# Turning the accumulated stick-breaking values by plain transposes, with the two halves added on VectorE

## The chip, the cores and the metric

The kernel runs on one core of one Trainium2 chip. Its metric is the device time of one execution in microseconds (us), taken as the median of several executions. The changed kernel is measured in the same way. Within the core, TensorE multiplies matrices into PSUM (its partial-sum memory), VectorE and ScalarE read PSUM and work on SBUF (the core's working memory), GpSimd works on SBUF, and SyncE's queue issues the transfers between DRAM and SBUF. In the rows of the profile these are PE (with PEld for its weight loads), DVE, ACT, POOL and SP.

## The reference, cut to what matters

The reference is one layer of a decoder over 2048 tokens of width 1024. A normalised input is projected to the inputs of four mixers. Their outputs are normalised, put side by side and projected back. A feed-forward part (gate, up and down products) follows. The change lies in one mixer, the stick-breaking attention with four heads of width 64:

```python
z = einsum('bqhd,bkhd->bhqk', qblk, kh) * scale
log_1m = where(causal, log_sigmoid(-z), 0.0)
tail = cumsum(log_1m, reverse=True) - log_1m
w = where(causal, exp(log_sigmoid(z) + tail), 0.0)
out = einsum('bhqk,bkhd->bqhd', w, vh)
```

For every query the keys before it are weighted, and `out` is the weighted sum of the values. The kernel reaches float32 accuracy with a faster rounded number format by carrying each operand as two parts, a rounded high part and a remainder.

## The kernel before, in words

The program has two stages. In the first, up to about 780 us, the projections and the four mixers run interleaved. In the second come the output projection and the feed-forward part. The change touches only the first.

The stick-breaking attention (function `stick`) is called 8 times: for 2 pairs of heads, and in each pair for 4 chunks of 512 queries. One call walks over its 2 heads and, for each, over the blocks of 512 keys from the nearest back to the first. For each block:

- `weights` multiplies queries by keys into a PSUM tile `z` (L325, L326). ScalarE takes two sigmoids (L329 into `tfix`, L332 into `s`). VectorE forms the running product with a scan (L338, tile `pr`) and multiplies (L343).
- `turn` transposes the weights with TensorE (L353, tile `tr`, four transposes of 128x128 at a time). ScalarE writes the high part (L355) and VectorE the remainder (L356), tile `wt`.
- `values` multiplies by the stacked values (L364, L365) and accumulates in a PSUM tile `acc`. The values of one head are held as 128 columns, 64 of the high part and 64 of the remainder, so `acc` has 128 rows: the sum for the high part above the sum for the remainder.

After the last block of a head, `finish` runs. ScalarE copies `acc` to SBUF (L371, tile `accs`). TensorE multiplies each 128 queries of it by `stack`, two identities of 64 one above the other (L374): this turns the tile and adds its two halves in one product. The result `yp` (128 queries by 4 times 64) is copied by ScalarE into `ysb` (L376). Two heads and 4 chunks in 2 pairs make 16 calls of `finish`. `acc` and `yp` share one PSUM bank: their pool tag has a single buffer, so the next head's `acc` cannot start before `yp` has been read. At the end of a call, two transfers store `ysb` to DRAM (`yd<-ysb`).

`stick` is one generator of work. A second one, `feed`, yields the projections and the other mixers, and `merge` draws from both with a ratio for each call. That gives the order of the program. A scheduler of the framework then reorders the instructions of each engine by its own estimate of times, so a changed instruction can move others far away from it. All transfers go through one issuing queue in order (L121). In the rows, `ps<-h,w_k` and the like are projections (L265 to L267, L277 to L279); `z<-ck,cq` (L468), `o<-block` (L510) and the loads `qr<-cd` and `kr<-cd` belong to the sliding-window mixer, whose operands GpSimd splits (L460, L461, tile `cq`).

Of the kernel before, what the change touches and what calls it, by code (L numbers as in the profile page):

```python
# [9 lines left out]
F32 = mybir.dt.float32  # L10
F32R = mybir.dt.float32r
AF = mybir.ActivationFunctionType
ALU = mybir.AluOpType
PSUM = bass.MemoryType.PSUM

P = 128
# [5 lines left out]
HD = 64  # L22
# [15 lines left out]
def _t5_bucket(dist):  # L38
    df = np.maximum(dist, 1).astype(np.float32)
    large = 16 + (np.log(df / np.float32(16)) / np.float32(math.log(8.0)) * np.float32(16)).astype(np.int32)  # L40
    return np.where(dist < 16, dist, np.minimum(large, 31))


def _constants():
    c = {}
    c["ident"] = np.eye(P, dtype=np.float32)
    c["ones"] = np.ones((P, P), np.float32)
    c["stack"] = np.concatenate([np.eye(HD, dtype=np.float32)] * 2, 0)
    j = np.arange(384)
    dist = 255 - j  # L50
    inside = (dist >= 0) & (dist < P)
    b = _t5_bucket(np.clip(dist, 0, P - 1))
    oh = np.zeros((32, 384), np.float32)
    oh[b[inside], j[inside]] = 1.0
    c["onehot"] = oh
    c["outside"] = np.where(inside, 0.0, NEG).astype(np.float32)[None, :]

    tok, out = np.arange(P)[:, None], np.arange(P)[None, :]
    band, first, before = (np.zeros((P, 2, 2, n), np.float32) for n in (P, P, 16))
    for g, w in enumerate((2, 4, 8, 16)):  # L60
        inside = ((out >= tok) & (out - tok < w)).astype(np.float32)
        band[:, g // 2, g % 2] = inside / np.float32(w) - (out == tok)
        first[:, g // 2, g % 2] = inside / np.minimum(out + 1, w).astype(np.float32) - (out == tok)
        before[:, g // 2, g % 2] = ((out + P - tok < w) / np.float32(w))[:, :16]
    c["band"] = np.concatenate([band.reshape(P, -1), before.reshape(P, -1)], 1)
    c["band0"] = first.reshape(P, -1)
    return c


def _layout(inputs):  # L70
# [30 lines left out]
    for n, v in _constants().items():  # L101
        a["c_" + n] = v
# [9 lines left out]
def build(nc, tc, A):  # L112
    with ExitStack() as top:
        _build(nc, tc, A, top)


def _build(nc, tc, A, top):
    V, S, G = nc.vector, nc.scalar, nc.gpsimd

    def load(out, in_):  # L120
        nc.sync.dma_start(out, in_)  # L121
# [19 lines left out]
    ident = const.tile([P, P], F32, name="ident")  # L141
# [28 lines left out]
    with ExitStack() as ph1:  # L170
        fas = ExitStack()
        fa = fas.enter_context(tc.tile_pool(name="feeda", bufs=2, side="left", reuse_waits="tile"))
        c1 = ph1.enter_context(tc.tile_pool(name="c1", bufs=1, side="left"))
        sb = ph1.enter_context(tc.tile_pool(name="sb", bufs=2, side="left"))

        stack = c1.tile([P, HD], F32, name="stack")
        tfix = [c1.tile([P, CH + 1], F32, name=f"tfix{i}") for i in range(2)]
        for t in tfix:
            G.memset(t[:, CH:CH + 1], 1.0)
# [133 lines left out]
        def stick(c, pair, q):  # L313
            ysb = sb.tile([P, 4, 2, HD], F32, name="ysb", tag="ysb", bufs=1)
# [44 lines left out]
            def values(h, j, kb, r, wt):  # L359
                vs = vstack[:, 4 * j + kb, h, :]  # L360
                first = j == c and kb == 0
                if first:
                    acc[h] = psum.tile([P, CH], F32, name="acc", tag="acc", bufs=1)
                nc.tensor.matmul(acc[h][:, r], vs, wt[:, 0, r], start=first, stop=False)  # L364
                nc.tensor.matmul(acc[h][:, r], vs, wt[:, 1, r], start=False, stop=j == 0 and kb == 3)  # L365
                if j == 0 and kb == 3:
                    finish(h)

            def finish(h):
                accs = sb.tile([P, CH], F32, name="accs", tag="accs", bufs=1)  # L370
                S.copy(accs, acc[h])  # L371
                yp = psum.tile([P, CH], F32, name="yp", tag="acc", bufs=1)
                for i in range(4):
                    nc.tensor.matmul(yp[:, i * HD:(i + 1) * HD], accs[:, i * P:(i + 1) * P], stack,  # L374
                                     start=True, stop=True)
                S.copy(ysb[:, :, h, :], yp[:, :4 * HD].rearrange("p (i d) -> p i d", d=HD))  # L376

            groups = [(h, j) for h in range(2) for j in range(c, -1, -1)]
            prev, late = None, None
# [356 lines left out]
        def new_q():  # L736
            return [sb.tile([P, 2, CH], F32R, name="dq", tag="dq", bufs=4) for _ in range(2)]
# [44 lines left out]
        def feed():  # L782
# [9 lines left out]
            w_v = split_w(A["w_v"], "w_v", "wv", 1)  # L792
            w_b = [split_w(A["w_b"][:, 4 * t:4 * t + 4], f"w_b{t}", eng=V, k0=4 * t) for t in range(2)]
            spare.clear()
            load(stack, A["c_stack"])
            q[0] = new_q()
            pool = mixer_b()
            for s in range(NS):
                c = s // 2
# [6 lines left out]
                h = hs.pop(s) if s else hs.pop(0)  # L806
# [72 lines left out]
            for s in range(NS):  # L879
                h = hs.pop(s)  # L880
# [16 lines left out]

        sw = []
        source = feed()
        reached = [0]  # L900

# [24 lines left out]
        for n in range(2 * NCH):  # L926
            c, pair = n % NCH, n // NCH
# [206 lines left out]
```

## Time and profile before

| | |
|---|---|
| median of 3 runs | 2396.13 us (2395.85 to 2400.73) |
| the profiled execution's own time | 2402.21 us |
| its span | 2400.5 us |
| mean granted TensorE clock | 0.974 of full speed |
| TensorE busy in the span | 2271.7 us (95%) |
| VectorE busy | 1505.8 us (63%) |
| ScalarE busy | 1024.8 us (43%) |
| first stage, mixers | up to about 780 us |

The profiled execution is 6.1 us above the median of the runs, so a sum made from its rows is a difference to be taken from the median. A share of busy time is a mean over stages: TensorE is near full use in the second stage, while the first has waits on VectorE and on transfers. The granted clock is given as a share of full speed (2.4 GHz); 0.5 is the lower of its two levels.

### The profile page before, as it was taken

The numbers are of one execution on the slowest core, as the hardware profiler recorded it, in microseconds if no ns is written. First come the engines' busy times: TensorE is split into PE (matmuls) and PEld (weight loads), VectorE is DVE, ScalarE is ACT, GpSimd is POOL, SyncE is SP. The second block draws the span as 40 slices with busy tenths as digits, with TensorE's granted clock in tenths as the row PEclk, the third lists the DMA queues.
The fourth block names the chain that finished last, engine by engine and source line by source line (L and its number), as shares of the span: only waits on it lengthen the run. The fifth ranks groups of instructions, "written<-read, shape, count | busy, mean of one in ns | idle before, by whom it ended". The sixth has DMA issues, their size and how long they took to land.

```text
span 2400.5 us, 31011 instructions
## 1 busy us (share of the span) xinstructions
PE 2271.7 (95%) x11432; PEld 1915.6 (80%) x11432; DVE 1505.8 (63%) x2467; ACT 1024.8 (43%) x2176; POOL 278.8 (12%) x356
## 2 busy tenths in 40 slices
PE   6999999998977899989999999999999999999998
PEld 6989888887865787768888888888888888888886
DVE  4356989887675455567666666644576666653443
ACT  5556656664455243343333333533333333333332
POOL 4222423441122120100000000000000000000000
PEclk9999999998977999999999999999999999999999
DMA  7534322333532245753222223665432222234553
GB/s 278 190 130 171 139 89 88 106 103 112 192 105 91 100 139 162 234 186 98 91 92 80 79 79 125 200 201 168 146 104 84 79 86 89 87 107 141 186 174 123
DMA packets 141001, 314.05 MB, mean 131 GB/s; under 512 B 12688, under 2 KB 68400, under 8 KB 134704
## 3 DMA queue, kind: packets, MB, share of 16 engines
q1 hardware_dynamic: 140848, 312.06, 38.8%
q8 instruction: 90, 1.47, 0.2%
q14 instruction: 63, 0.52, 0.1%
HBM read 229.44 MB, written 82.58 MB: 130 GB/s over the span
## 4 chain that ended last, share of the span: by engine, by line
PE 73%; DMA 10%; DVE 8%; ACT 4%; issue 3%; POOL 2%; SPq 1%; DVEq 0%; POOLq 0%; ACTq 0%
PE dn L1081 20%; PE gb L1025 15%; PE gc L1025 10%; PE ga L1025 10%; DVE pr L338 2%; PE ops L728 2%; PE ops L730 2%; PE ops L729 2%; DMA y<-yd 1%; DVE s L343 1%; DMA qr<-cd 1%; DMA xt<-in_x 1%; PE ps L277 1%; PE ps L278 1%; PE ps L279 1%
## 5 line engine op out<-in xcount | busy, mean ns | idle before, releaser
L1081 PE MATMUL dn<-wd,act 128*128 128x512 f32 x2112 | 479.5, 389 | 0.0
L1081 PEld LDWEIGHTS dn<-wd,act 128*128 128x128 f32 x2112 | 396.5, 188 | 82.4
L1025 PE MATMUL gb<-T,fw 128*128 128x512 f32 x1584 | 388.2, 394 | 0.0
L1025 PEld LDWEIGHTS gb<-T,fw 128*128 128x128 f32 x1584 | 297.5, 188 | 68.5
L1025 PE MATMUL ga<-B,fw 128*128 128x512 f32 x1056 | 259.5, 394 | 0.0
L1012 ACT CAST fw<-fsum 128x512 fp32r<-128x512 f32 x176 | 108.4, 619 | 308.4 <-DVE fsum L1008 162.3
L1025 PEld LDWEIGHTS ga<-B,fw 128*128 128x128 f32 x1056 | 198.6, 188 | 45.9
L975 DVE TENSOR_TENSOR wd<-wr,wd 128x512 fp32r<-128x512 f32 x176 | 115.2, 689 | 186.4 <-ACT wd L1075 186.2
L1075 ACT CAST wd<-wr 128x512 fp32r<-128x512 f32 x176 | 102.0, 619 | 236.5 <-DMA wr<-in_w_down 208.8
L149 POOL TENSOR_TENSOR fr<-rs_t,mhalf 128x1 f32<-128x1 f32 x32 | 21.5, 674 | 1433.1 <-DVE rs_t L148 1428.2
L975 DVE TENSOR_TENSOR fw<-fsum,fw 128x512 fp32r<-128x512 f32 x176 | 120.9, 690 | 36.4 <-ACT fw L1012 36.0
L1025 PE MATMUL gc<-T,fw 128*128 128x512 f32 x528 | 131.6, 397 | 5.8 <-DVE T L975 5.8
L338 DVE TENSOR_TENSOR_SCAN pr<-tfix,cr 128x513 f32<-128x513 f32 x96 | 126.1, 1323 | 11.4 <-ACT tfix L329 11.1
L1025 PE MATMUL gc<-B,fw 128*128 128x512 f32 x528 | 128.0, 391 | 0.0
L1025 PEld LDWEIGHTS gc<-T,fw 128*128 128x128 f32 x528 | 100.6, 191 | 28.7 <-DVE T L975 6.2
L728 PE MATMUL ops<-wo,yT 128*128 128x512 f32 x256 | 105.7, 413 | 11.5 <-ACT yT L656 10.8
L1025 PEld LDWEIGHTS gc<-B,fw 128*128 128x128 f32 x528 | 99.2, 188 | 21.7
L343 DVE TENSOR_TENSOR s<-s,pr 128x512 f32<-128x512 f32 (+3 forms) x152 | 107.9, 717 | 10.8 <-POOL s L335 4.5
L356 DVE TENSOR_TENSOR wt<-tr,wt 128x512 fp32r<-128x512 f32 (+3 forms) x160 | 94.1, 601 | 29.5 <-ACT wt L355 29.3
L1012 ACT CAST fw<-fraw 128x512 fp32r<-128x512 f32 x132 | 81.7, 621 | 66.9 <-DVE fw L975 32.4
L730 PE MATMUL ops<-wo,yT 128*128 128x512 f32 x256 | 102.7, 407 | 3.4 <-DVE yT L657 3.4
L729 PE MATMUL ops<-wo,yT 128*128 128x512 f32 x256 | 104.2, 408 | 0.0
(234 smaller groups left out, 4499.0 us busy)
## 6 DMA issues: line engine op xcount, KB each, us to landing
fraw<-in_w_gu SPq DMA_DIRECT2D x88, 512.0 KB
wr<-in_w_down SPq DMA_DIRECT2D x88, 512.0 KB
h<-hd SPq DMA_DIRECT2D x32, 1024.0 KB
actd<-up SPq DMA_DIRECT2D x88, 256.0 KB
ar<-actd SPq DMA_DIRECT2D x88, 256.0 KB
hd<-h SPq DMA_DIRECT2D x16, 1024.0 KB
xr<-in_xT SPq DMA_DIRECT2D x16, 512.0 KB
xt<-in_x SPq DMA_DIRECT2D x16, 512.0 KB
```

The lines of the kernel that those rows point to most:

```text
L277: nc.tensor.matmul(o, hk[:, 0], w(k, 0), start=k == 0, stop=False)
L338: V.tensor_tensor_scan(pr[:, c0:][:, ::-1], t[:, c0:][:, ::-1], t[:, c0:][:, ::-1], carry[h][i], op0=ALU.mult, op1=ALU.bypass)
L343: (G if (4 * pair + c, i) in ON_G else V).tensor_tensor(w[:, c0:], w[:, c0:], pr[:, c0 + 1:], op=ALU.mult)
L356: V.tensor_tensor(wt[:, 1, r], tr[:, r], wt[:, 0, r].bitcast(F32), op=ALU.subtract)
L728: nc.tensor.matmul(ps, yk[:, 0, :], wo[k][half][:, 0], start=k == 0, stop=False)
L729: nc.tensor.matmul(ps, yk[:, 0, :], wo[k][half][:, 1], start=False, stop=False)
L730: nc.tensor.matmul(ps, yk[:, 1, :], wo[k][half][:, 0], start=False, stop=k == KT - 1)
L975: V.tensor_tensor(dst, src, hi.bitcast(F32), op=ALU.subtract)
L1012: S.copy(w[:, 0], src)
L1025: nc.tensor.matmul(bank, w[:, wi, sl], hc[n][:, k, hi], start=start and k + wi + hi == 0, stop=stop and k == 3 and wi == 1, skip_group_che ...
L1075: S.copy(w[n][:, 0], wr[:, n])
L1081: nc.tensor.matmul(pss[2 * i + n], a[:, ai, t], w[n][:, wi], start=f + ai + wi == 0, stop=f == NF - 1 and ai == 1)
```

## The change

The four products with `stack` (64 columns each) become four transposes of 128x128 with the identity, which is in SBUF anyway for `turn`. `yp` then holds, for each 128 queries, 64 columns of the high sum and 64 of the remainder's. ScalarE copies the first half into `ysb`, as wide as before, reading runs of 64 columns. VectorE then adds the second half from PSUM. The tile `stack`, its constant and its transfer go.

```diff
-    c["stack"] = np.concatenate([np.eye(HD, dtype=np.float32)] * 2, 0)
...
-        stack = c1.tile([P, HD], F32, name="stack")
...
                 S.copy(accs, acc[h])
                 yp = psum.tile([P, CH], F32, name="yp", tag="acc", bufs=1)
                 for i in range(4):
-                    nc.tensor.matmul(yp[:, i * HD:(i + 1) * HD], accs[:, i * P:(i + 1) * P], stack,
-                                     start=True, stop=True)
-                S.copy(ysb[:, :, h, :], yp[:, :4 * HD].rearrange("p (i d) -> p i d", d=HD))
+                    nc.tensor.transpose(yp[:, i * P:(i + 1) * P], accs[:, i * P:(i + 1) * P], ident)
+                ypv = yp.rearrange("p (i u d) -> p i u d", i=4, u=2)
+                S.copy(ysb[:, :, h, :], ypv[:, :, 0])
+                V.tensor_tensor(ysb[:, :, h, :], ypv[:, :, 1], ysb[:, :, h, :], op=ALU.add)
...
-            load(stack, A["c_stack"])
```

The scheduler moves other work too. On VectorE the order of the multiplication of `wraw` (L250) and of `dg` (L206), from which `rbc` is made, is exchanged near the start. Lines of the changed kernel stand 1 or 2 lower than the same lines before. Three places matter later.

On the transfers' queue, near the start of the program: loads of weights (`wraw`) and of the input (`xr`, `xt`), and the store of a row of scales (`rbcd<-rbc`, made by ScalarE). Before:

```order
L121 DMA stack<-in_c_stack 128x64
L121 DMA cw<-in_pool_w 64x64
L121 DMA hd_0_76<-h 128x2048
...
L121 DMA wraw<-in_w_b 128x1024
L121 DMA xr<-in_xT 128x4x256
L121 DMA rbcd_193<-rbc 128x256
L121 DMA xr<-in_xT 128x4x256
L121 DMA vd_68<-vt 128x2x256
```

And now:

```order
L120 DMA cw<-in_pool_w 64x64 x2
L120 DMA hd_0_76<-h 128x2048
...
L120 DMA wraw<-in_w_b 128x1024
L120 DMA rbcd_193<-rbc 128x256
L120 DMA xr<-in_xT 128x4x256 x2
L120 DMA xt<-in_x 128x1024
```

The load of `stack` is gone, a second small load of `cw` now stands ahead of the stores of `h`, and the first load of `xr` stands behind the store of `rbc`.

On VectorE at the 14th `finish` (about 625 us before); `pr` is the scan, `s` the product after it, `st` a projection's result. Before:

```order
L356 TENSOR_TENSOR wt<-tr,wt 128x512
L356 TENSOR_TENSOR wt<-tr,wt 128x384
L885 TENSOR_TENSOR st<-ps,rbc 128x256
L338 SCALAR_TENSOR_TENSOR pr<-tfix_221,cr 128x513
L343 TENSOR_TENSOR s<-s,pr 128x512
L338 SCALAR_TENSOR_TENSOR pr<-tfix_222,cr 128x513
L885 TENSOR_TENSOR st<-ps,rbc 128x256
```

And now:

```order
L354 TENSOR_TENSOR wt<-tr,wt 128x512
L354 TENSOR_TENSOR wt<-tr,wt 128x384
L883 TENSOR_TENSOR st<-ps,rbc 128x256
L336 SCALAR_TENSOR_TENSOR pr<-tfix_220,cr 128x513
L341 TENSOR_TENSOR s<-s,pr 128x512
L336 SCALAR_TENSOR_TENSOR pr<-tfix_221,cr 128x513
L375 TENSOR_TENSOR ysb<-yp,ysb 128x4x64
L336 SCALAR_TENSOR_TENSOR pr<-tfix_220,cr 128x513
```

The new addition stands between two scans, and the instruction behind it is a scan on which the next weights wait.

On TensorE at the 13th `finish` (about 571 us before), with the sliding-window products `z<-ck,cq` around it. Before:

```order
L353 MATMUL tr<-ident,s 128x128 x2
L468 MATMUL z<-ck,cq 128x128 x2
L468 MATMUL z<-ck,cq 128x256 x2
L325 MATMUL z<-kstack_226,dq 128x512
L326 MATMUL z<-kstack_226,dq 128x512
L353 MATMUL tr<-ident,s 128x128 x2
L468 MATMUL z<-ck,cq 128x128
L468 MATMUL z<-ck,cq 128x256
L325 MATMUL z<-kstack_226,dq 128x512
L326 MATMUL z<-kstack_226,dq 128x512
L374 MATMUL yp<-stack,accs 128x64 x4
L468 MATMUL z<-ck,cq 128x128 x3
```

And now:

```order
L351 MATMUL tr<-ident,s 128x128 x2
L323 MATMUL z<-kstack_225,dq 128x512
L324 MATMUL z<-kstack_225,dq 128x512
L351 MATMUL tr<-ident,s 128x128 x2
L467 MATMUL z<-ck,cq 128x128 x3
L263 MATMUL ps<-h,w_c 128x256
L264 MATMUL ps<-h,w_c 128x256
L265 MATMUL ps<-h,w_c 128x256
L323 MATMUL z<-kstack_225,dq 128x512
L324 MATMUL z<-kstack_225,dq 128x512
L372 MATMUL yp<-ident,accs 128x128 x4
L467 MATMUL z<-ck,cq 128x256 x4
```

The sliding-window products stand later and in larger groups, with projections `ps<-h,w_c` between them (21 more of these stand a little ahead of the piece shown).

## Rows read from the trace of the kernel before

**Rows 1.** The page, part 1: busy time of each engine.

```profile
PE 2271.7 (95%) x11432; PEld 1915.6 (80%) x11432; DVE 1505.8 (63%) x2467; ACT 1024.8 (43%) x2176; POOL 278.8 (12%) x356
```

**Rows 2.** Windows: length, then PE, PEld, DVE, ACT, POOL busy, clock, DMA share, GB/s.

```profile
60.00:270.00 210.00, 204.71 (x1382) 192.33 (x1381) 124.30 (x209) 126.66 (x293) 52.70 (x62) 0.98 0.44 155
270.00:540.00 270.00, 254.23 (x1538) 220.06 (x1537) 239.21 (x414) 170.88 (x395) 106.07 (x128) 1.00 0.31 105
```

**Rows 3.** Chain of work that ended last: start, length, what.

```profile
13.33 9.05 DMA wraw<-in_w_v
...
106.86 0.92 PE yp L374 x8
...
206.00 0.44 PE tr L353 x4
...
496.17 0.84 PE yp L374 x8
...
752.89 0.87 PE tr L353 x4
758.92 1.72 PE yp L374 x8
760.66 0.38 ACT ysb L376
```

**Rows 4.** Groups by shape: busy us, mean ns, idle before and releaser.

```profile
L338 DVE TENSOR_TENSOR_SCAN pr<-tfix,cr 128x513 f32<-128x513 f32 x96 | 126.1, 1323 | 11.4 <-ACT tfix L329 11.1
L353 PE MATMUL tr<-ident,s 128*128 128x128 f32 x544 | 95.2, 281 | 9.3 <-DVE s L343 5.1 <-DVE wt L356 4.0
L343 DVE TENSOR_TENSOR s<-s,pr 128x512 f32<-128x512 f32 x104 | 84.5, 820 | 4.5 <-ACT s L332 1.5 <-POOL s L335 0.8
L374 PE MATMUL yp<-stack,accs 128*128 128x64 f32 x128 | 17.1, 278 | 3.5 <-ACT accs L371 3.5
L285 DVE TENSOR_TENSOR sc<-ps,rbc 128x256 f32<-128x256 f32 x32 | 13.2, 416 | 3.1 <-PE ps L267 2.9
L371 ACT COPY accs<-acc 128x512 f32<-128x512 f32 x16 | 9.5, 596 | 0.0
L376 ACT COPY ysb<-yp 128x256 f32<-128x256 f32 x16 | 6.2, 386 | 3.5 <-PE yp L374 3.3
```

**Rows 5.** The chain of 270 to 540 us, its shares by line.

```profile
by line: DVE pr L338 15.9%; issue 14.7%; DVE s L343 9.7%; PE ps L277 6.0%; DVE wt L356 5.8%; PE ps L278 5.8%; PE ps L279 5.7%; PE tr L353 3.3%; POOL rv L149 2.1%; PE acc L365 2.0%; DVE gq L539 1.9%; DVE wraw L250 1.8%; PE acc L364 1.6%; DVE
```

**Rows 6.** Timeline around the transfers' queue's start, and around VectorE's `dg` there.

```profile
10.53 0.60 SPq L121 DMA_DIRECT2D cw<-in_pool_w  x1
...
24.27 1.23 DVE L250 TENSOR_TENSOR wraw<-wraw,gmix 128x1024 f32<-128x1024 f32 x1 [0.77 <-DMA wraw<-in_w_b]
25.41 2.03 DVE L206 TENSOR_SCALAR dg<-ident,rx 128x128 f32<-128x128 f32 x2
27.18 0.38 SPq L121 DMA_DIRECT2D xr<-in_xT  x1
28.44 0.33 SPq L121 DMA_DIRECT2D rbcd<-rbc  x1
```

**Rows 7.** Timeline at two finishes: the copy of `yp`, the next `acc`.

```profile
466.13 0.38 ACT L376 COPY ysb<-yp 128x256 f32<-128x256 f32 x1 [0.90 <-PE yp L374]
468.70 0.40 PE L364 MATMUL acc<-wt,vstack 128*128 128x512 f32 x1
...
625.40 0.37 ACT L376 COPY ysb<-yp 128x256 f32<-128x256 f32 x1
626.58 0.39 PE L364 MATMUL acc<-wt,vstack 128*128 128x512 f32 x1
```

**Rows 8.** Timeline of TensorE, 565 to 577 us: first and last of four waits.

```profile
565.75 0.50 PE L468 MATMUL z<-ck,cq 128*128 128x128 f32 x2 [1.69 <-POOL cq L460]
...
576.08 0.69 PE L468 MATMUL z<-ck,cq 128*128 128x128 f32 x2 [1.60 <-POOL cq L461]
```

**Rows 9.** Window of 10 us, columns as in rows 2.

```profile
570.00:580.00 10.00, 6.76 (x38) 6.29 (x38) 10.00 (x13) 3.30 (x10) 4.82 (x5) 0.75 0.13 43
```

## The prediction

> **What bounds the kernel now.** I read the page's busy times first: TensorE works 95% of the span [rows 1], so whatever TensorE saves looks like time. The busy share is a mean over stages, so I then read the windows of the first stage, the only one that the change touches. From 60 to 270 us TensorE is busy 204.7 of 210 us and VectorE 124.3. From 270 to 540 us both are near full: 254.2 and 239.2 of 270 us [rows 2]. The reader is to see that a saving on TensorE and an addition on VectorE weigh differently in the two stretches. Third, the chain of work that ended last, looked through for the 16 finishes. It passes through the products `yp` in only five of them: four at the full clock (first and last shown, 0.92 and 0.84 us; the two between take 0.84 and 0.92), and the 16th at the lower clock (1.72 us) [rows 3]. At the other eleven it runs elsewhere. Fourth, the chain of 270 to 540 us by line: scan 15.9%, product behind it 9.7%, remainder of `wt` 5.8%, so VectorE carries at least 31% of that stretch [rows 5]. So TensorE limits the finishes early, VectorE takes a large part in the middle, and the last finish lies wholly on the chain.
>
> **The change part by part.**
>
> *TensorE.* Before, one finish costs 0.84 to 0.92 us of TensorE's time on the chain; the row has eight instructions, since each of the four products runs as two passes (128 records for 64 products) [rows 3, 4]. After, a finish has four transposes of the form that `turn` uses, which run as one pass each (544 records); four cost 0.44 us at the full clock and 0.87 us at the lower one [rows 3, 4]. Four finishes on the chain save 3.52 - 4 x 0.44 = 1.8 us. The 16th saves 1.72 - 0.87 = 0.9 us. The eleven others save 11 x 0.44 = 4.8 us of TensorE's time (0.88 less 0.44 each), of which between nothing and all reaches the end. I take 1.5 us, about a third, since they lie in stretches where TensorE is nearly full but shares the chain. Together 4.2 us saved, between 2.7 and 7.5.
>
> *ScalarE.* The copy stays 256 elements wide (386 ns) but reads runs of 64 out of 512. No row shows that form. If it cost as much as a copy of all 512 (596 ns) it would add 16 x 0.21 = 3.4 us on an engine that is busy 171 of 270 us in its fuller stretch [rows 2, 4]; a gain has no reason, as the element count is the same. I take nothing on the path, and 0.2 us at the last finish as the upper end.
>
> *VectorE.* 16 additions of 256 elements, one operand in PSUM. The nearest row is the scaling of a projection, also 256 elements with PSUM: 416 ns [rows 4]. That makes 6.7 us of busy time. Seven finishes (2.9 us) lie between 270 and 540 us, where VectorE carries 31% of the chain: 0.9 us. Before 270 us the chain is rarely on VectorE, so I count nothing; the cover is its idle time of 86 us in 210, and without it 5 x 0.42 = 2.1 us come on top. The last addition stands between the copy and the store of `ysb`, both on the chain [rows 3]: 0.42 us and a hand-over of about 0.05, so 0.5 us. Together 1.4 us lost, between 0.5 and 6.7.
>
> The addition is also a new wait. On VectorE the 14th stands between two scans, and behind it is the scan that the next weights need. The bank of `yp` is free for the next `acc` only when the addition is done. Before, the copy was the last reader, and the nearest next product came 0.81 us (626.58 less 625.77) and 2.19 us (468.70 less 466.51) after it; two rows are shown for the tightest places [rows 7]. I cost the delay at nothing because the copy now comes 0.44 us earlier, which pays for the addition itself if VectorE takes it at once; the price if it doesn't is in the rivals.
>
> *The transfers' queue.* The load of `stack` goes, and was hidden. What moves is dearer. A second load of `cw`, about 0.60 us on the queue, now stands ahead of the `wraw` load at 13.33 us, which the startup's chain waits for [rows 3, 6]. The first load of `xr`, issued at 27.18 us, now waits behind the store of `rbc`, issued at 28.44 us. If `rbc` comes when it came, `xr` loses 28.44 + 0.33 - 27.18 = 1.6 us. But `dg`, from which `rbc` is made, started only at 25.41 us behind a multiplication of 1.23 us, and that now stands behind it [rows 6]; `rbc` should come about 1.1 us earlier. So the startup loses between nothing and 0.6 + 1.6 = 2.2 us; I take 1.0.
>
> *TensorE's order.* In the middle, sliding-window products stand later and in larger groups with projections between. Before, TensorE waited four times between 565 and 577 us, 1.6 to 1.7 us each, 6.6 us in all [rows 8], and that slice ran at a granted clock of 0.75 [rows 9]. The new order puts work there, yet what TensorE waits for (transfers, GpSimd) may then be late elsewhere. The value lies between -3.3 us (half of the waits) and +3.3; with no row for it I take nothing.
>
> *The sum.* -4.2 + 1.4 + 1.0 = -1.8 us against the profiled execution, 2402.2 to 2400.4 us. That execution stood 6.1 us above the median of the runs, so on their scale 2396.1 - 1.8 = 2394.3 us. A measurement of this kernel can tell about 0.2%, 4.8 us, from no change: my forecast is that no difference shows.
>
> **A rule that speaks against the change.** In rows, `turn` issues 544 transposes, 95 us of TensorE's time, and the stretches that hold most of them have granted clocks of 0.98 and 1.00 [rows 2, 4]. The Trainium skill, "TensorE: Matmul & The Clock Gate", Part 4 (PE-mode transpose), says that transposes don't count as TensorE activity in the way products do, so that the clock isn't raised for them. By that rule, 64 fewer activity-giving products could let the clock fall; the trace agrees only so far that it does not exclude it, since transposes there always stand beside products. As a mechanism of this kernel, it would act where a finish has waits around it. A slice at 0.75 gives away a quarter of 10 us, 2.5 us [rows 9]. If this came at the four finishes of the chain that run at the full clock, it would cost 10 us and give 2404 us. A finish is 0.44 us in slices of 10 us that are full of products, so I give it 5%.
>
> **The rivals.**
>
> *All of the saving arrives (faster).* TensorE is 95% busy; the whole 7.5 us come off, and the new order fills half of the four waits (3.3). Less the last addition (0.5), the middle ones (0.9) and the startup (1.0): -8.4 us, 2387.7 us. For it speaks the window of 60 to 270 us, with TensorE 97% busy; against it that the chain passes through only five finishes and that VectorE is 89% busy from 270 us on [rows 2, 3]. 25%.
>
> *VectorE becomes the bound (slower).* The additions queue behind scans. One that waits for a scan and a product (1.32 + 0.82) and takes 0.42 ends 2.56 us after the copy, so the next `acc` is late by 1.75 us where 0.81 were free and by 0.37 where 2.19 were, 2.1 us in all [rows 4, 7]. Every addition then also holds up the scan behind it, 6.7 us. With the startup's 1.3 us and only the chain's own 2.7 us saved: +7.4 us, 2403.5 us. It decides from the point where an addition ends more than about 0.8 us later than the copy did. For it speaks VectorE's 239 of 270 us; against it that half of the finishes lie elsewhere. 22%.
>
> *The forecast*, 2391 to 2400 us, has 48%, and the clock 5%.
>
> **How the numbers follow.** Below 2391.3 us (faster by over 0.2%) lie 23 of the first rival's 25% and 7 of the forecast's 48: 0.30. Above 2400.9 us lie 18 of the 22, 4 of the 5 and 2 of the 48: 0.24. The rest, 0.46, is within 0.2%. The range for 8 in 10 runs from a little below the first rival's time to a little above the second's and the clock's, 2386 to 2405 us; the forecast's own is 2391 to 2400.
>
> **What would show it.** Right: rows of four one-pass transposes with 0.4 to 0.5 us on the chain, additions near 0.42 us, the end of the first stage within a few us of before, a startup about 1 us longer, TensorE's busy time less by 7 us with about as much idle time in its place. Wrong towards faster: the waits near 570 us gone and the clock at 1.00 there. Wrong towards slower: waits of TensorE for `ysb` by VectorE ahead of the first `acc` product, scans late behind additions, or new slices with a clock below 1. What would make the whole prediction wrong is a change of order that moves a long transfer onto or off the chain, which I cannot price from these rows.

## The result, and the profile after

The changed kernel took 2418.88 us (median of 4 runs, 2415.78 to 2422.11), the kernel before 2398.43 us beside it (4 runs, 2395.85 to 2401.03). The ratio is 1.0074, 95% interval 1.0054 to 1.0095: slower by 13 to 23 us. I had forecast 2394.3 us, no difference that shows, in a range up to 2405. The forecast was wrong, in sign and beyond its range.

The parts that I had sized from rows came out as sized. The groups by shape of the changed kernel (busy us, mean ns of one, idle time before and its releasers):

```profile
L336 DVE TENSOR_TENSOR_SCAN pr<-tfix,cr 128x513 f32<-128x513 f32 x96 | 130.8, 1373 | 5.0 <-ACT tfix L327 4.9
L372 PE MATMUL yp<-ident,accs 128*128 128x128 f32 x64 | 10.4, 287 | 4.4 <-ACT accs L369 4.4
L375 DVE TENSOR_TENSOR ysb<-yp,ysb 128x256 f32<-128x256 f32 x16 | 6.5, 409 | 5.3 <-ACT ysb L374 5.2
L374 ACT COPY ysb<-yp 128x256 f32<-128x256 f32 x16 | 6.1, 381 | 2.2 <-PE yp L372 2.1
```

The products of the 16 finishes fell from 17.1 us [rows 4] to 10.4 us in all, the copy stayed (6.2 to 6.1 us), and the additions took 6.5 us, with 5.2 us in which VectorE stood before them for ScalarE's copy. None of this is near 20 us. The windows of the first stage show more (columns as in [rows 2]):

```profile
60.00:270.00 210.00, 199.81 (x1349) 187.65 (x1348) 125.35 (x214) 125.12 (x291) 51.08 (x62) 0.97 0.44 155
270.00:540.00 270.00, 252.72 (x1442) 219.46 (x1442) 231.58 (x400) 161.35 (x369) 104.75 (x126) 0.95 0.29 99
```

From 270 to 540 us TensorE is as busy as before (252.7 against 254.2 us) but has run 96 instructions fewer, and the granted clock is 0.95 where it was 1.00 [rows 2]. VectorE, which the additions should have filled, is less busy (231.6 against 239.2). Something was late, and TensorE also ran slowly.

Where the time goes is seen from one event that both kernels have 16 times, the start of ScalarE's copy `accs<-acc`, and from the first products `ops` and `gb` of the second stage. The table gives the profiled time less that of before, in us.

| profile of | 1st | 4th | 6th | 9th | 12th | 16th | first `ops` | first `gb` |
|---|---|---|---|---|---|---|---|---|
| before (its times) | 104.5 | 211.3 | 306.9 | 446.7 | 525.3 | 758.3 | 777.9 | 1049.2 |
| after | -4.4 | 1.5 | 9.1 | 13.6 | 20.8 | 9.2 | 16.1 | 20.0 |

The start is early, 19 us are lost between the 4th and the 12th finish, 11.6 come back by the 16th, and 10.8 are lost again up to the first `gb`. The additions alone couldn't do that. The order of all the work had changed, and this was the term to test first.

### The profile page after: what moved, and what is told of

It is laid out like the page before. It is cut to its first block, busy times and chain, and to the rows that moved or that the text cites. A ratio compares the mean times of both kernels' runs of the same rounds, so it can differ in the third digit from the quotient of the medians.

```text
span 2419.7 us, 30913 instructions
## 1 busy us (share of the span) xinstructions
PE 2275.5 (94%) x11368; PEld 1919.0 (79%) x11368; DVE 1515.2 (63%) x2483; ACT 1026.8 (42%) x2176; POOL 274.5 (11%) x356
## 4 chain that ended last, share of the span: by engine, by line
PE 78%; DVE 8%; DMA 6%; ACT 3%; issue 3%; POOL 1%; SPq 1%; DVEq 0%; POOLq 0%; ACTq 0%
PE dn L1079 20%; PE gb L1023 15%; PE gc L1023 10%; PE ga L1023 10%; DVE pr L336 3%; PE ops L727 2%; PE ps L275 2%; PE ps L276 2%; PE ps L277 2%; PE ops L729 2%; PE ops L728 2%; DMA y<-yd 2%; PE ps L263 2%; PE ps L264 1%; PE ps L265 1%
## 5 line engine op out<-in xcount | busy, mean ns | idle before, releaser
L727 PE MATMUL ops<-wo,yT 128*128 128x512 f32 x256 | 106.3, 415 | 21.9 <-ACT yT L655 21.9
L351 PE MATMUL tr<-ident,s 128*128 128x128 f32 x544 | 98.8, 287 | 12.2 <-DVE wt L354 8.4
L729 PE MATMUL ops<-wo,yT 128*128 128x512 f32 x256 | 103.2, 410 | 2.9 <-DVE yT L656 2.9
```

The costliest lines, as they stand in the source:

```text
L351: nc.tensor.transpose(tr[:, i * P:(i + 1) * P], wq[i][:, col:col + P], ident)
L727: nc.tensor.matmul(ps, yk[:, 0, :], wo[k][half][:, 0], start=k == 0, stop=False)
L729: nc.tensor.matmul(ps, yk[:, 1, :], wo[k][half][:, 0], start=False, stop=k == KT - 1)
```

## The experiments

All ratios are against the kernel before on the same chip, 5 rounds each; 0.1% is 2.4 us. "Old instructions" are those of before, "new" those of the changed kernel. To give one kernel's instructions another's order, the order on each engine was fixed by links between neighbours that make the scheduler keep it and add no wait on the chip:

```diff
         build(nc, tc, A)
+        _pin(nc, tc)
...
+        for x, y in zip(order[:-1], order[1:]):
+            tc.add_manual_dep(traced[int(y)], traced[int(x)].name, info, reason="order")
```

| run | instructions, order | ratio | 95% interval |
|---|---|---|---|
| `old_in_new` | old, order of the changed kernel | 1.0055 | 1.0043 to 1.0067 |
| `new_in_old` | new, order of before | 1.0051 | 1.0039 to 1.0063 |
| `noadd_in_new` | new without additions, order of the changed kernel | 1.0046 | 1.0033 to 1.0058 |
| `noadd_in_old` | new without additions, order of before | 1.0002 | 0.9993 to 1.0010 |
| `new_placed` | new, order of before, additions moved | 1.0031 | 1.0019 to 1.0043 |
| `spin_in_old` | as `new_in_old`, additions that wait for nothing | 1.0005 | 0.9997 to 1.0014 |
| `sbuf_add_in_old` | additions from SBUF, bank freed by ScalarE | 1.0026 | 1.0015 to 1.0037 |
| `gp_add_in_old` | the same on GpSimd | 1.0049 | 1.0035 to 1.0062 |
| `old_new_first` | old, changed order up to the 12th finish | 1.0036 | 1.0024 to 1.0048 |
| `old_new_last` | old, changed order after the 12th finish | 1.0048 | 1.0036 to 1.0059 |
| `old_new_to4` | old, changed order up to the 4th finish | 0.9993 | 0.9984 to 1.0003 |
| `old_new_4to12` | old, changed order from the 4th to the 12th | 1.0052 | 1.0036 to 1.0069 |
| `old_in_new_y` | `old_in_new`, one move on the queue | 1.0034 | 1.0021 to 1.0047 |
| `after_y` | changed kernel, same move | 1.0048 | 1.0035 to 1.0061 |
| `old_4to12_wt` | `old_new_4to12`, four moves on VectorE | 1.0037 | 1.0024 to 1.0051 |
| `after_y_wt` | `after_y`, the same four moves | 1.0029 | 1.0019 to 1.0038 |
| `after_stack` | changed kernel with an idle load: another order | 1.0064 | 1.0047 to 1.0080 |
| `noadd_free` | new without additions, a third order | 0.9995 | 0.9985 to 1.0005 |

**Order or additions?** The first four runs cross the two. Each addition stood in the old order where ScalarE's copy stood. Theory O says that the order did it, theory V that VectorE with its additions did it.

> The kernel before, instruction for instruction (products with the stacked identities, no addition), but every engine issues in the order of the changed kernel. Theory O: about the changed kernel's time, 2412 to 2424 us. Theory V: about the time of the kernel before, 2394 to 2403 us.

> The changed kernel's instructions (four transposes, copy, addition on VectorE, no load of the stacked identities), but every engine issues in the order of the kernel before; each addition stands on VectorE at the place where the copy of yp stood among all instructions. Theory O (the order did it): the instructions cost nothing to speak of, so the time is that of the kernel before within 0.2% (2394 to 2403 us when before is 2398). Theory V (VectorE did it: the additions and the later release of the PSUM bank): the time stays near the changed kernel, 2413 to 2422 us.

> As new_in_old, but the 16 additions are left out, so the second half of the accumulated values is missing from the output. Theory O: 2391 to 2400 us, and no more than 3 us below new_in_old. Theory V: 2390 to 2396 us, and 15 us or more below new_in_old.

> The changed kernel in its own order, but the 16 additions are left out, so the second half of the accumulated values is missing from the output. TensorE waited for the additions twice, 3.8 us together. Theory O: 2409 to 2420 us, at most 6 us below the changed kernel. Theory V: 2394 to 2403 us.

Each theory holds for a part. The order alone, with not one instruction changed, costs 0.55%, some 13 us. The additions alone, in the order of before, cost 0.51 - 0.02 = 0.49%, some 12 us. The transposes by themselves cost or give nothing (1.0002): 6.7 us less work on TensorE did not show at the end. In the changed kernel's own order the additions cost less, 0.74 - 0.46 = 0.28%, about 7 us. Fixing an order costs nothing by itself that shows: the old instructions with every place fixed, and only the start in the changed order, took 0.9993 (`old_new_to4` below).

**What of an addition costs?** VectorE spends 6.7 us on them in the old order, so most of the 12 us had to be a wait. The trace of `new_in_old` has it (answer for the line of the addition: what its engine waited for, and who waited for it):

```profile
L375 DVE TENSOR_TENSOR ysb<-yp,ysb x16: 397/419/425, 109.1 to 769.3; 128x256 f32<-128x256 f32 x16
...
  ACT ysb L374: 11.0, 6
who waited for it (us, times):
  PEld acc L362: 3.5, 4
  PE acc L362: 2.6, 2
```

At six finishes VectorE reached the addition before ScalarE's copy was done and stood 11.0 us, with scans and remainders queued behind; at two, TensorE waited 2.6 us for the bank. Two runs separate the time on VectorE from the wait and the held bank. The edit on VectorE

```diff
-L375 ysb<-yp,ysb 128x4x64
 L336 pr<-tfix 128x129
 L625 yb<-po,cw 128x2x128
+L375 ysb<-yp,ysb 128x4x64
```

is the first of the eight places that `new_placed` moves, and `spin_in_old` has, for each addition, a stand-in of as many elements that waits for nothing and holds no bank (`idb` is the identity, read twice)

```diff
-                V.tensor_tensor(ysb[:, :, h, :], ypv[:, :, 1], ysb[:, :, h, :], op=ALU.add)
+                V.tensor_tensor(spin, idb, idb, op=ALU.add)
```

> The new instructions in the order of before, the additions put by the trace: where VectorE stood waiting for ScalarE's copy (1st, 2nd, 3rd, 7th, 9th) 1 to 4 instructions later, where the addition came long after the copy and held the bank (5th, 6th, 14th) one earlier. With each addition at the place of the old copy the kernel took +13 us, of which VectorE idled 11.0 us at six additions and TensorE waited 2.6 us for the bank. Theory 'the wait at the head of VectorE's queue costs': +2 to +6 us (2404 to 2408). Theory 'the time on VectorE costs' (16 x 0.42 = 6.7 us, plus what it pushes): +10 to +13 us (2412 to 2415).

> The new instructions in the order of before, but each addition is replaced, at the same place, by one of 256 elements on a constant in SBUF that waits for nothing and holds no bank (the second half of each value is not added). Without any addition this order takes +0.5 us. Theory 'VectorE's time costs': +6 to +13 us. Theory 'the wait for the copy and the bank cost': 0 to +4 us.

```profile
L377 DVE TENSOR_TENSOR spin<-ident 128x256 bf16<-128x256 f32 x16 | 8.1, 506 | 0.0
```

VectorE's time costs nothing that shows: the 16 stand-ins took 8.1 us of it (mean 506 ns), more than the additions, and the ratio is 1.0005. So the price lies in what the additions wait for and hold. Moved places halve VectorE's waiting, from 11.0 to 5.2 us, and bring the price from 12 to 7 us, while TensorE's wait for the bank rose from 2.6 to 3.4 us. So VectorE's wait is a large part, though neither theory's figure for `new_placed` was met in full. Was the rest the bank? In `sbuf_add_in_old`, and with `G` for `V` in `gp_add_in_old`, `ypv` is a view of `accs`:

```diff
-                S.copy(ysb[:, :, h, :], ypv[:, :, 0])
-                V.tensor_tensor(ysb[:, :, h, :], ypv[:, :, 1], ysb[:, :, h, :], op=ALU.add)
+                S.copy(accs, yp)
+                V.tensor_tensor(ysb[:, :, h, :], ypv[:, :, 1], ypv[:, :, 0], op=ALU.add)
```

> The new transposes in the order of before; ScalarE copies all of yp (both halves) back into accs, and VectorE adds the halves from there, at the places of the kernel that took +7.5 us (1 to 4 instructions later where VectorE had waited for the copy). So the bank comes free when ScalarE's copy ends, and not when VectorE's addition does. Theory 'what was left was the bank held by the addition': 0 to +3 us against before. Theory 'what was left was VectorE's wait for the copy and what the addition pushes': +5 to +8 us, as with the operand in PSUM.

> As the kernel with the copy of both halves, but the addition is GpSimd's, in GpSimd's order at the place of the old copy. VectorE has none of the change. Both theories of VectorE (its wait, the bank) say 0 to +3 us, as with no addition at all (+0.5). If GpSimd then stands waiting for copies and the operands of the sliding-window products come later: +4 us or more.

No gain shows: with the bank freed by ScalarE it is 1.0026, not told apart from 1.0031. The run is no clean test of the bank, as ScalarE's copy of both halves takes 0.59 us at the median instead of 0.37, and VectorE still waits 3.1 us for it; what the last 6 or 7 us are stays open. With GpSimd it is 1.0049. Its row suggests why: at eight additions GpSimd stood 40.6 us for ScalarE's copy. What came late behind it isn't shown.

```profile
L375 POOL TENSOR_TENSOR ysb<-accs x16: 723/809/1745, 111.8 to 769.7; 128x256 f32<-128x256 f32 x16
...
  ACT accs L374: 40.6, 8
```

**Where does the order cost?** First by halves, then by stretches.

> The old instructions; up to the 12th finish (about 525 us) each engine issues them in the order of the changed kernel, after it in the order of before. In the run with the new order throughout, the finishes 10 to 12 come 11 to 13 us later than before, then the 16th only 2 us later, and the second stage's first products again 9 to 13 us later. Theory 'lost where the order is new and carried on': about +13 us (2415). Theory 'the middle's loss is taken up again by transfers that TensorE waits for anyway between 620 and 760 us, and what stays lost arises at the change of stages': 0 to +4 us (2402 to 2406).

> The old instructions; up to the 12th finish in the order of before, after it in the order of the changed kernel. Theory 'lost in the middle and carried on': 0 to +3 us (2402 to 2405). Theory 'lost at the change of stages': +8 to +13 us (2410 to 2415), with two waits of the output products for yT of over 7 us each where before has one, and a wait of the sliding-window products for block of about 11 us where before has 4.1.

Either half costs most of the whole: 0.36 and 0.48% against 0.55 together. Both theories are thus half right. What is late in the first half is partly made up by the 16th finish: `old_new_first` is 13.7 us late at the 12th and 6.4 us at the 16th. TensorE's idle time in between is only 2.5 us less than in before (44.0 for 46.5), so that waits which it has anyway take up all of it isn't shown.

The second half has one place. From the 16th copy `accs` to the first `ops`, before takes 19.6 us; the five runs with the changed order in this stretch (the changed kernel, `old_in_new`, `noadd_in_new`, `old_new_last`, and `after_stack` with its own) take 26.3 to 27.0. All transfers go through one queue in order. Its rows in before, and then in the changed kernel (start, length of the issue with its waits, what):

```profile
740.20 7.43 SPq L121 DMA_DIRECT2D qr<-cd  x4
751.47 1.03 SPq L121 DMA_DIRECT2D kr<-cd  x2
757.34 1.18 SPq L121 DMA_DIRECT2D qr<-cd  x2
761.06 1.04 SPq L121 DMA_DIRECT2D yd<-ysb  x2
...
762.88 0.43 SPq L121 DMA_DIRECT2D y<-yd  x1
```

```profile
752.55 11.53 SPq L120 DMA_DIRECT2D qr<-cd  x4
764.19 4.30 SPq L120 DMA_DIRECT2D kr<-cd  x2
773.41 1.22 SPq L120 DMA_DIRECT2D qr<-cd  x2
774.68 3.54 SPq L120 DMA_DIRECT2D yd<-ysb  x2
...
779.00 0.43 SPq L120 DMA_DIRECT2D y<-yd  x1
```

The queue has the same transfers in the same order. But a load of `qr` or `kr` waits there until its buffer is empty. With this wait the four loads of `qr` take 11.53 us of the queue instead of 7.43. The two of `kr` take 4.30 instead of 1.03 and the two stores 3.54 instead of 1.04, for which no row gives a reason. GpSimd's rows show where the waits end, in before (first row) and in the changed kernel (the others):

```profile
750.04 1.41 POOL L461 TENSOR_TENSOR cq<-qr,cq 128x256 fp32r<-128x256 f32 x2
```

```profile
761.61 1.42 POOL L460 TENSOR_TENSOR cq<-qr,cq 128x256 fp32r<-128x256 f32 x2
...
771.98 1.41 POOL L460 TENSOR_TENSOR cq<-qr,cq 128x256 fp32r<-128x256 f32 x2
```

In the changed kernel the second two of the four `qr` go at 763.05 us, when GpSimd has split the first two (763.03), and the last two at 773.41, when it has split the second two (773.39). GpSimd itself had waited 5.8 and 5.7 us for these transfers. In before the second two went at 746.60 us, 4.9 us before the first two were split (751.45), and only the loads behind them waited for GpSimd. Why this buffer came free late in the changed order isn't shown. So `y`, the input of the second stage, is issued 6.9 us after the next product `o` has ended (772.15); in before it went as that product ended. The chain of the changed kernel shows the same from its side, the last finish as well:

```profile
768.13 1.13 PE yp L372 x4
...
769.69 0.44 DVE ysb L375
...
770.17 1.98 PE o L509 x8
...
779.00 6.67 DMA y<-yd
```

The test moves the last two `qr` behind the first loads of `y`:

```diff
 kr<-cd_190 128x1x256 x2
-qr<-cd_190 128x1x256 x2
 yd_66<-ysb, yd_67<-ysb, gffn, y<-yd_60, xres, y<-yd_60, xres
+qr<-cd_190 128x1x256 x2
```

> The old instructions in the order of the changed kernel, with one move on the transfers' queue: the last two loads qr<-cd of the first stage go from ahead of the stores yd<-ysb, the load of gffn and the first two loads each of y and xres to behind them. In that order without the move the queue stood at four loads of qr for 11.97 us (7.43 in before) and then at two of kr for 4.08 (1.03), so that the first y<-yd was issued at 772.41 us, 7.0 us after TensorE's last product that it also waits for (before: at 762.88, at once). Theory 'the queue delays the second stage': the first y<-yd at 765 to 767 us, and 5 to 7 us less than that order's +0.55% of its time, so +6 to +8 us against before. Theory 'what the second stage waits for lies elsewhere': no change, +13 us.

> The changed kernel in its own order with the same move on the transfers' queue (first y<-yd at 779.00 us, 6.9 us after the end of the product o<-block at 772.15). Theory 'queue': 5 to 7 us less than the changed kernel's +18 us, so +11 to +13 us against before. Theory 'elsewhere': +18 us.

```profile
757.37 4.14 SPq L120 DMA_DIRECT2D kr<-cd  x2
763.32 2.13 SPq L120 DMA_DIRECT2D yd<-ysb  x2
...
766.22 0.43 SPq L120 DMA_DIRECT2D y<-yd  x1
```

That is `after_y`: `y` goes out 766.22 us into the program, and from the 16th `accs` to the first `ops` it takes 20.2 us (`old_in_new_y` 20.4) instead of 26.5 and 27.0. The medians give back 0.26% (6 us) with the new instructions and 0.21% (5 us) with the old. Each pair's intervals overlap a little, but the place and the 6 to 7 us agree in both: the queue is shown.

The first half has no single place.

> The old instructions in the order of before, except up to the 4th finish (about 211 us), where they stand in the order of the changed kernel. With that order up to the 12th finish the time was +8.7 us. In the profiles with the new order the first finish comes 3 to 5 us earlier than before and the 4th 1 to 2 us earlier or as early. Theory 'the start is no loss': -5 to +1 us. Theory 'what the prediction said of the startup's queue' (a loss of up to 2.2 us there, or what it leaves behind): +1 to +4 us.

> The old instructions in the order of before, except between the 4th and the 12th finish (211 to 525 us), where they stand in the order of the changed kernel. Theory 'the stretch in which VectorE is nearly full loses, by waits for VectorE and by slices with a granted clock of 0.83 to 0.95 where before has 1.00': +7 to +12 us. Theory 'it is the start that is paid for later': 0 to +4 us.

The start is no loss (0.9993), so my startup term had the wrong sign, if any. The stretch from the 4th to the 12th finish costs 0.52% with the old instructions. Its window of 210 to 530 us, in before, in `old_new_4to12` and in the changed kernel (columns as in [rows 2]):

```profile
210.00:530.00 320.00, 304.84 (x1879) 268.26 (x1879) 278.94 (x466) 205.69 (x478) 119.74 (x144) 1.00 0.32 109
```

```profile
210.00:530.00 320.00, 301.39 (x1813) 265.47 (x1812) 268.10 (x452) 196.98 (x458) 113.72 (x139) 0.97 0.29 100
```

```profile
210.00:530.00 320.00, 300.54 (x1758) 264.01 (x1756) 271.97 (x455) 194.64 (x451) 112.76 (x138) 0.95 0.28 98
```

The clock falls with the order. A mean of 0.95 over 320 us is at most as much work lost as TensorE does in 16 us at full speed (0.05 x 320). TensorE's idle time rises less, from 15.2 us to 18.6 and 19.5, so by these rows more of the loss is slow work than waiting. The mean is uncertain: `after_y`, with the changed kernel's order in this window, has 0.97. What comes first is a wait. TensorE's waits in that window, in before and in the changed kernel (us in all, times, longest):

```profile
PE acc L365 <- DVE wt L356: 7.0, 7, 1.6
```

```profile
PE tr L351 <- DVE wt L354: 5.8, 2, 3.4
PE acc L363 <- DVE wt L354: 3.7, 4, 2.7
```

Before waits often and shortly, up to 1.6 us in this line and 2.2 in any. The changed kernel has waits of 3.4 and 2.7 us. The longest, in its timeline:

```profile
509.42 2.39 POOL L250 TENSOR_TENSOR w_c<-wraw,w_c 128x1024 fp32r<-128x1024 f32 x1 [1.23 <-ACT w_c L249]
509.89 3.01 DVE L336 TENSOR_TENSOR_SCAN pr<-tfix,cr 128x513 f32<-128x513 f32 x1
...
513.88 1.74 DVE L336 TENSOR_TENSOR_SCAN pr<-tfix,cr 128x513 f32<-128x513 f32 x1
515.55 0.66 DVE L354 TENSOR_TENSOR wt<-tr,wt 128x512 fp32r<-128x512 f32 x1
...
516.36 0.66 PE L351 MATMUL tr<-ident,s 128*128 128x128 f32 x2 [3.39 <-DVE wt L354]
```

A scan that takes 1.28 us at the median (of 96 in either kernel) takes 3.01 beside GpSimd's 128x1024 operation: it ends 1.1 us after that one has ended. Then another scan, then the remainder `wt` that TensorE needs. The Trainium skill ("SBUF — State Buffer", section "SBUF: two separate sides") says that VectorE, with two inputs in SBUF, and a GpSimd operation that reads SBUF take a shared pair of ports as an exclusive lock, and the loser waits for the whole instruction. This trace agrees: 1.1 us, most of a scan's time, lie behind the operation's end, and `wt`, with an operand in PSUM, stays under 0.70 us in all its rows. Before has such scans too:

```profile
266.61 2.40 POOL L252 TENSOR_TENSOR w_q<-wraw,w_q 128x1024 fp32r<-128x1024 f32 x1 [4.50 <-ACT w_q L251]
...
267.05 3.04 DVE L338 TENSOR_TENSOR_SCAN pr<-tfix,cr 128x513 f32<-128x513 f32 x1 [0.57 <-ACT tfix L329]
```

but behind this one TensorE's longest wait is 1.5 us (at 274.28), and its `w_c` at 507.72 us meets no scan. What the wait leads to is in the windows of 5 us of the changed kernel:

```profile
507.00:512.00 5.00, 5.00 (x27) 3.78 (x26) 5.00 (x8) 4.74 (x10) 3.44 (x4) 1.00 0.54 156
512.00:517.00 5.00, 1.38 (x9) 1.09 (x8) 4.89 (x6) 3.01 (x7) 2.54 (x2) 0.76 0.00 0
517.00:522.00 5.00, 4.44 (x23) 3.99 (x22) 5.00 (x8) 3.38 (x9) 2.00 (x4) 0.55 0.02 3
```

TensorE is busy 1.38 of 5 us, the clock falls to the lower of its two levels (0.5), and the next 5 us of work run at 0.55. So the wait is paid twice: once as idle time, then as slow work. The last two runs move the awaited instructions ahead of the long ones, at 264 us and likewise `wt` at 279 and 513 us, and `kstack`, `dq` and `sc` at 411:

```diff
 L354 wt<-tr,wt 128x512
+L354 wt<-tr,wt 128x384
 L302 kstack_224<-sc,kstack_224 64x256
 L302 kstack_225<-sc,kstack_225 64x256
-L354 wt<-tr,wt 128x384
```

> The old instructions, in the changed kernel's order between the 4th and the 12th finish and in before's elsewhere (+12.5 us), with four moves on VectorE: the remainder wt that TensorE waits for goes ahead of two kstack<-sc (at 264 us in the changed kernel), ahead of a scan (279), ahead of a product and a scan (513), and kstack, dq and the two sc ahead of two scans (411). Theory 'these waits and the low clock behind them are the loss': TensorE's waits of 2.0, 2.5 and 3.0 us there go, the granted clock of the stretch rises from 0.97 to 0.99 or 1.00, and 6 to 12 us come back (0 to +6 us against before). Theory 'the waits move to the next place': less than 3 us come back.

> The changed kernel with the move on the transfers' queue (+11.5 us) and the same four moves on VectorE. Theory 'waits and clock': 6 to 10 us come back, so +1 to +6 us against before: the changed kernel within 0.2% of before by order alone. Theory 'the waits move to the next place': +9 to +12 us.

About a third came back, some 4 us, between the two theories. From the 4th to the 12th finish the old instructions now take 325.1 us instead of 329.6 (before: 314.0), the new ones 325.8 instead of 329.0, and the clock of the stretch is 0.98 for 0.97 in both. One profile of this stretch says little: the same order took 328.4 and 333.1 us there (`old_in_new`, `old_in_new_y`), 333.2 and 329.0 (the changed kernel, `after_y`). But all seven profiles with the changed order there lie between 327.0 and 333.2 us, and both profiles with the moves lie below these. The medians fell by 0.15 and 0.19%, with overlapping intervals. The waits at 268 and 412 us are gone; the one behind the two scans went from 2.95 to 2.62 us, as another `wt` is next there; those at 448 (for ScalarE's `s`) and 469 us (for `sc`) were not moved. So waits and clock are a part of the loss, as both pairs point the same way. That they are all of it is not shown.

**Any order, or this one?** Two kernels were left to the scheduler: the changed kernel with one load more, of which nothing reads, and the changed kernel without its additions.

```diff
+            load(stack, A["c_stack"])
```

```diff
-                V.tensor_tensor(ysb[:, :, h, :], ypv[:, :, 1], ysb[:, :, h, :], op=ALU.add)
```

> The changed kernel with the load of the tile stack left in, which nothing reads any more. The work is the same; the scheduler makes another order of it (about as far from the changed kernel's as from before's). Theory 'one unlucky order': +5 to +12 us (what the additions cost in the order of before is +7 to +12 us). Theory 'any new order of these instructions loses its chains of transfers': +14 to +22 us, as the changed kernel (+18).

> The transposes without the additions (the second half of each value is not added), in the order that the scheduler makes for them by itself. In the order of before these instructions took +0.5 us, in that of the changed kernel +11 us. Theory 'any new order loses': +6 to +14 us. Theory 'one unlucky order': -5 to +4 us.

The same work in another order (`after_stack`) is 1.0064, not told apart from 1.0074. Without the additions, the order that the scheduler makes is 0.9995, and its clock from 210 to 530 us is 1.00 again:

```profile
210.00:530.00 320.00, 303.51 (x1864) 265.65 (x1864) 281.26 (x472) 203.26 (x473) 116.64 (x143) 1.00 0.32 110
```

So not every new order loses; with the additions both did.

## Why the prediction was wrong

- **The step that failed: "TensorE's order".** I gave it between -3.3 and +3.3 us and took nothing, "with no row for it". Measured with the old instructions it is +13 us. About 5 us of it came back by one move on the transfers' queue and about 4 us by four moves on VectorE; the rest has no named place. I had looked at the one place of the order where before waited [rows 8], for what a new order could fill there, and not at what it could open elsewhere. My last sentence named a danger close to what happened at the change of stages (a "long transfer onto or off the chain") and gave it no chance. The load of `y` was on the chain before as well (6.69 us, from 762.88 us); it did not come onto the chain but started late on it.
- **VectorE's term was mis-sized.** I took 1.4 us and at most 6.7, the busy time. The additions cost about 12 us in the old order and 7 in the new. The rival "VectorE becomes the bound" had the right parts, additions that queue and a bank that comes free late, but priced an addition that waits for a scan. The dear case is the reverse: a scan that waits behind an addition, which waits for ScalarE's copy. The busy time itself costs nothing that shows. (That rival's sum also takes 1.3 us for the startup where the forecast takes 1.0; with 1.0 it is 2403.2 us, which changes no chance.)
- **TensorE's 4.2 us did not arrive.** Without additions and in the old order the transposes are at 1.0002 (0.9993 to 1.0010), where the least that I allowed, 2.7 us, would be 0.9989. The work itself shrank nearly as sized (6.7 us of the 7.5; at the last finish 1.13 us instead of 1.72, where I had taken 0.87). So the reading of the chain as a sum of savings was wrong: in the profile of that run the 16th finish comes 1.2 us later than before, with the savings of the first 15 behind it. Where they went isn't shown; a saving ahead of a transfer or of a wait for VectorE may be waited away there.
- **Startup: +1.0 us taken, 0.9993 measured**, which is within 0.2%. The load of `wraw` that I saw pushed back went at 12.56 us instead of 13.33, the first `xr` at 28.11 instead of 27.18, and the first finish came 4 us earlier in the profile.
- **The last finish was right**: the addition is on the chain with 0.44 us and the hand-over.
- **The clock did fall, but not by the rule that I weighed.** With all 64 transposes of the finishes, in its own order, `noadd_free` has the stretch at 1.00; with not one of them, in the changed order, `old_new_4to12` has it at 0.97. In that run it fell behind waits of TensorE for VectorE of 2.0 to 3.0 us, in the changed kernel of up to 3.4. Not every such wait has a fall behind it: before stayed at 1.00 with one of 2.2 us (at 528 us). To a fall of the clock I had given 5%, for the other reason.

## What to carry to other kernels

When a small edit makes a scheduler reorder the program, the order is a change of its own, here worth as much as the edit; hold the order fixed to measure the edit, and run the old instructions in the new order to measure the order. An instruction put on an in-order engine can cost far more by what that engine waits at its head than by what it takes: look for whether its operand is ready when the engine gets there. Where one queue issues all transfers, a load that waits for a buffer delays every load behind it, so what the next stage needs goes ahead of loads with slow buffers.

## What the runs showed of the hardware that was not expected

- VectorE's scans and products with all operands in SBUF take up to 3.4 us (a scan at 279.48 us of the changed kernel) instead of 0.7 to 1.3 when they meet a GpSimd operation of 128x1024; the remainder `wt`, which reads PSUM, never takes over 0.70 us in the changed kernel's 160 rows.
- After a wait of 3.39 us the granted clock was 0.55 for the next 5 us of work, though TensorE had been busy for all of the 5 us from 507 to 512 us, ahead of the wait (the changed kernel).
- Four 128x128 transposes with the identity are one pass each, 0.27 us at the median; the 64-column float32 products that they replace are two passes each, 0.28 us a pass.
- 8.1 us more on VectorE, 89% busy in the middle of the first stage [rows 2], cost nothing measurable when nothing waits (1.0005, 0.9997 to 1.0014).
